# Down by seven block products for eight, with a contraction that rolls over slots

## The chip, the cores and the metric

The kernel runs on one core of a Trainium2 chip. The metric is the device time of one execution in microseconds (us), as the median of several. PE is TensorE (matmuls), DVE is VectorE, ACT is ScalarE, and SyncE's queue (SP) issues the DMAs between the chip's DRAM and its on-chip memory. PE's results land in PSUM, which has eight banks of 512 fp32 columns.

## The reference, cut to what matters

One layer of a streaming encoder, in fp32, for 1024 positions of width 1024. What the change touches is its end, the MLP:

```python
h2 = rms_norm(x, norm2_g)                                        # (1024, 1024)
u = jnp.square(jax.nn.relu(jnp.einsum('bsd,df->bsf', h2, w_up)))  # (1024, 4096)
x = x + jnp.einsum('bsf,fd->bsd', u, w_down)                      # (1024, 1024)
```

I call the product with w_up *up* and the product with w_down *down*.

## The kernel before, in words

Everything lies transposed: channels on the 128 partitions, positions along a row. The stages follow each other on PE: attention with the first gates, the conv branch with the other gates, its projection (cp), the attention's projection (ap), out, up, down. An fp32 product is made from three matmuls: each operand is *cut* into a high part (an ACT cast, `split`, L81) and the rest (a DVE subtraction, L82), and high x high, low x high and high x low add up in one PSUM bank. A matmul has 128 x 128 weights and 512 columns.

The gates, the conv branch and up use *seven block products for eight*. The operand on the right is held in four *slots*; slot j is two tiles of 128 channels by 1024 positions, thus four blocks of 128 x 512, and `slot` makes seven operands of them: blocks 1 to 4 as they are or differences of them. `weights` fetches four weight blocks (a11, a12, a21, a22, 256 KB each), makes sums of them with four DVE operations and cuts seven operands. A product, numbered 1 to 7 and taken in the order 1, 2, 6, 7, 5, 4, 3 (`ORDER`), sums over the four slots: 4 x 3 = 12 matmuls. One job of 84 matmuls yields 256 output channels by 1024 positions. In `product` the first and the last job of a phase are "wide": slot by slot, all seven products side by side in seven banks. The others go product by product in three banks, and ACT or DVE read the banks in between.

Up is 16 jobs (`up_job`). Its results are squared relus, written by DVE and sent to DRAM as 32 tiles uD. Down is plain (`plain`): four quarters of the contraction, each with eight tiles uk loaded from uD (512 KB, through three staging buffers, `bw.stg`) and cut, and eight output tiles, 48 matmuls for each output tile and half-row pair. The quarters are summed in acc by DVE (L1091 to L1107). The last quarter also applies the norm's factor ms and adds to the residual.

The order of the work on each engine is fixed when the program is built: a scheduler lays out each engine's instructions in one queue, and an instruction waits at the head of its queue until its inputs are there and its buffer is free. Buffers come from pools with a fixed count per tag (bufs). SyncE's DMAs stand in one such queue.

Of the kernel before, what the change touches and what calls it, by code (L numbers as in the profile page):

```python
# [8 lines left out]
F32 = mybir.dt.float32  # L9
# [31 lines left out]
def block_kernel(ctx, tc, x, xt, wqkv, wcnv, wgate, wcp, wap, wout, wup, wdown,  # L41
# [135 lines left out]
    h2D = [dram.tile([P, S], F32, name=f"h2D{t}") for t in range(ND)]  # L177
    uD = [dram.tile([P, S], F32, name=f"uD{t}") for t in range(FF // P)]

# [439 lines left out]
    class Work:  # L619


        def __init__(self, name, e, stg, tt, side="right"):
            self.n = (e, stg, tt)
            self.pool = ctx.enter_context(tc.tile_pool(name=name, bufs=1, side=side))

# [3 lines left out]
        def stg(self, name):  # L629
            return self.pool.tile([P, S], F32, name=name, tag="stg", bufs=self.n[1])  # L630
# [44 lines left out]
    def from_dram(tiles, first=0):  # L675
        return lambda dst, kt: nc.sync.dma_start(dst, tiles[first + kt][:])
# [20 lines left out]
    def mms(ps, w, o, i, j, start, stop, chain):  # L697
        x = o[j]
        for n, (u, v) in enumerate(((0, 0), (1, 0), (0, 1))):
            matmul(ps[:], w[i][:, u, j, :], x[:, PROD[i][1], v, :], start and n == 0,  # L700
                   stop and n == 2, chain)
# [5 lines left out]

    def product(src, o, name, ev, wide=None, w=None):


        w = w or weights(src, name)
        if not wide:
            a = bank(f"pa_{name}")

            def whole(ps, i, start, stop):
                for j in range(4):
                    mms(ps, w, o, i, j, start and j == 0, stop and j == 3, True)
            whole(a, 1, True, True)
            if ev.sums:
# [202 lines left out]
    def plain(src, o, name, ev, lead=3, then=None, final=False):  # L922
# [90 lines left out]
    kbs.close()  # L1013
    jls = ExitStack()

    jul = [jls.enter_context(tc.tile_pool(name=f"jul{j}", bufs=1)) for j in range(2)]
    xos = ExitStack()
# [4 lines left out]
    def ev_out(t, c, ps):  # L1022
# [14 lines left out]
        if c == 1 and t in (1, 3):  # L1037
            h2o[t // 2] = slot((jul[t // 2], "js"), t // 2, "n", from_dram(h2D))
    plain(wout, mk, "o", ev_out)
    first = weights(wup[0], "u0")  # L1040
    xos.close()
    kas.close()
    jrs = ExitStack()
    for j in range(2, 4):
        jur = jrs.enter_context(tc.tile_pool(name=f"jur{j}", bufs=1, side="right"))
        h2o[j] = slot((jur, "js"), j, "n", from_dram(h2D))


# [22 lines left out]

    phase([up_job(i) for i in range(16)], h2o, (1, 2, 3, 0), first, 7, mean_square)
    jls.close()
    jrs.close()

    ktd = ctx.enter_context(tc.tile_pool(name="ktd", bufs=1, side="right"))
    acc = [[None] * 2 for _ in range(ND)]

    def ktile(pool, name):
        return pool.tile([P, 2, S], F32R, name=name, tag="kt", bufs=NKD)  # L1080
    NKD = 12
    accp = ctx.enter_context(tc.tile_pool(name="accp", bufs=1))
    acc = [accp.tile([P, S], F32, name=f"acc{t}") for t in range(ND)]
    for k in range(4):
        def uk(k=k):
            return ktiles(ktd, f"uk{k}_", uD, 8 * k)

        def ev_d(t, c, ps):
            a = acc[t][:, cols(c)]
            if k == 0:  # L1090
                nc.scalar.copy(a, ps[:])  # L1091
            elif k < 3:
                nc.vector.tensor_tensor(a, ps[:], a, op=ALU.add)
            if k == 2:

                x2 = bw.e(f"xr{t}_{c}")
                nc.sync.dma_start(x2[:], x2D[t][:, cols(c)])
                nc.vector.tensor_tensor(a, a, ms[:, cols(c)], op=ALU.mult)
                nc.vector.tensor_tensor(a, a, x2[:], op=ALU.add)
            if k == 3:  # L1100
                e = bw.e(f"xl{t}_{c}")
                n = 2 if t == ND - 1 and c else 1
                for q in range(n):
                    f = slice(q * HC // n, (q + 1) * HC // n)
                    g = slice(c * HC + f.start, c * HC + f.stop)
                    nc.vector.tensor_tensor(e[:, f], ps[:, f], ms[:, g], op=ALU.mult)
                    nc.vector.tensor_tensor(e[:, f], e[:, f], acc[t][:, g], op=ALU.add)  # L1107
                    nc.sync.dma_start(out[t * P:(t + 1) * P, g], e[:, f])
        plain(wdown[k], uk if k == 0 else uk(), f"d{k}_", ev_d, 3 if k else 1,
              None, k == 3)  # L1110


def _layout(inputs):
# [53 lines left out]
```

## Time and profile before

| | |
|---|---|
| median of 3 runs | 1810.55 us (1809.3 to 1812.17) |
| the profiled execution | 1811.89 us, span 1810.1 us |
| PE busy | 1785.5 us, 99% of the span |
| DVE busy | 1130.4 us, 62% |
| ACT busy | 695.6 us, 38% |
| up, from the span's start | about 1142 to 1450 us |
| down | about 1450 us to the end |

The span runs from the first to the last instruction on the core; the device time lies some 2 us above it. A row's busy time says what an engine did; an idle time beside it says what it waited for. Where PE is busy throughout, only PE's own rows and PE's waits say what the end depends on.

### The profile page before, as it was taken

To read this page: it belongs to the slowest core of one execution; us is meant where nothing else is said; L and a number is where in the kernel's file an instruction comes from. 1 tells how busy PE (TensorE), PEld (TensorE's weight loads), DVE (VectorE), ACT (ScalarE), POOL (GpSimd) and SP (SyncE) were. 2 spreads that over 40 slices of the span, in tenths; PEclk is the share of its full clock that TensorE was granted. 3 is DMA by queue.
4 is the path that set the end of the run, shared out by engine and by line. 5 is a ranking of instruction groups with operands and counts; after the bars stand their busy time and mean duration, and the time that the engine had idled before them with its cause. 6 is when DMAs were issued, how large, how long until landed. Compare 5 with 4: busy or idle time off the path is not lost.

```text
span 1810.1 us, 24728 instructions
## 1 busy us (share of the span) xinstructions
PE 1785.5 (99%) x8884; PEld 1543.2 (85%) x8884; DVE 1130.4 (62%) x2106; ACT 695.6 (38%) x1337; POOL 151.1 (8%) x419
## 2 busy tenths in 40 slices
PE   7999999999999999999999999999999989999999
PEld 7899999999888888888888888788888878888887
DVE  6777877787759766765543629975765452325532
ACT  6555555565534333333432414433333233212200
POOL 5232223222100000000000000000000000000000
PEclk9999999999999999999999999999999999999999
DMA  7443444433335332213673628543333262424311
GB/s 278 104 114 92 101 109 106 104 102 95 107 108 154 94 99 88 79 57 117 211 235 116 199 75 282 186 150 110 94 127 111 88 223 87 138 68 135 111 64 53
DMA packets 123692, 225.02 MB, mean 124 GB/s; under 512 B 13745, under 2 KB 30385, under 8 KB 123569
## 3 DMA queue, kind: packets, MB, share of 16 engines
q1 hardware_dynamic: 123424, 223.40, 40.2%
q8 instruction: 70, 1.15, 0.3%
q14 instruction: 54, 0.43, 0.1%
q10 hardware_dynamic: 144, 0.03, 0.0%
HBM read 147.88 MB, written 50.33 MB: 110 GB/s over the span
## 4 chain that ended last, share of the span: by engine, by line
PE 90%; DVE 3%; DMA 2%; issue 1%; ACT 0%; SPq 0%; DVEq 0%; ACTq 0%
PE ps_d L74 19%; PE psq L74 13%; PE pa_u L74 8%; PE ps_ap L74 5%; PE ps_cp L74 5%; PE ps_g L74 5%; PE pb_u L74 4%; PE av L74 4%; PE s L74 3%; PE tp L77 3%; PE pa_b L74 2%; PE pa_x L74 2%; PE pa_c L74 2%; PE p_g L74 2%; PE pc_u L74 2%; PE ps_o L74 2%
## 5 line engine op out<-in xcount | busy, mean ns | idle before, releaser
L74 PE MATMUL psq<-w_q,hT 128*128 128x384 f32 x1536 | 347.5, 351 | 9.3 <-ACT w_q L81 6.6
L74 PE MATMUL ps_d<-uk,w_d 128*128 128x512 f32 x1536 | 350.8, 391 | 4.9 <-DVE uk L82 3.9
L74 PEld LDWEIGHTS ps_d<-uk,w_d 128*128 128x128 f32 x1536 | 289.2, 188 | 66.4 <-DVE uk L82 4.7
L74 PEld LDWEIGHTS psq<-w_q,hT 128*128 128x128 f32 x1536 | 261.2, 192 | 12.9 <-ACT w_q L81 6.6
L74 PE MATMUL pa_u<-on,w_u 128*128 128x512 f32 x672 | 160.0, 390 | 0.1
L74 PEld LDWEIGHTS pa_u<-on,w_u 128*128 128x128 f32 x672 | 126.0, 188 | 27.1 <-ACT s_u L705 0.5
L82 DVE TENSOR_TENSOR w_d<-r_d,w_d 128x512 fp32r<-128x512 f32 x64 | 42.7, 687 | 143.4 <-ACT w_d L81 143.3
L400 ACT ACTIVATE p<-p,sm 128x640 f32<-128x640 f32 (+4 forms) x128 | 89.5, 699 | 74.3 <-DVE sm L398 70.5
L81 ACT CAST w_d<-r_d 128x512 fp32r<-128x512 f32 x64 | 38.8, 622 | 168.4 <-PE ps_d L74 160.7
L74 PE MATMUL ps_g<-hT,w_g 128*128 128x512 f32 x384 | 99.6, 398 | 0.7 <-DVE ao L454 0.7
L398 DVE CUSTOM_DVE_ANT_0 p<-s,b 128x640 f32<-128x640 f32 (+4 forms) x128 | 83.3, 651 | 13.0 <-PE s L74 12.6
L82 DVE TENSOR_TENSOR pt<-tp,pt 128x512 fp32r<-128x512 f32 (+1 forms) x144 | 84.2, 596 | 10.4 <-ACT pt L81 9.7
L74 PEld LDWEIGHTS av<-pt,vt 128*128 128x128 f32 x576 | 86.1, 188 | 2.4 <-DVE pt L82 0.6
L74 PE MATMUL av<-pt,vt 128*128 128x256 f32 (+1 forms) x576 | 87.8, 274 | 0.1
L74 PE MATMUL ps_cp<-yk,w_cp 128*128 128x512 f32 x384 | 87.2, 389 | 0.0
L74 PE MATMUL ps_ap<-ak,w_ap 128*128 128x512 f32 x384 | 87.2, 389 | 0.0
L74 PE MATMUL ps_o<-mk,w_o 128*128 128x512 f32 x384 | 87.2, 389 | 0.0
L74 PE MATMUL s<-k,q 128*128 128x384 f32 (+3 forms) x384 | 81.8, 322 | 4.7 <-DMA k<-kh 3.7
L81 ACT CAST pt<-tp 128x512 fp32r<-128x512 f32 (+1 forms) x144 | 71.8, 515 | 37.6 <-PE tp L77 37.3
L74 PEld LDWEIGHTS ps_cp<-yk,w_cp 128*128 128x128 f32 x384 | 72.1, 188 | 15.0
L74 PEld LDWEIGHTS ps_ap<-ak,w_ap 128*128 128x128 f32 x384 | 72.1, 188 | 15.0
L74 PEld LDWEIGHTS ps_o<-mk,w_o 128*128 128x128 f32 x384 | 72.1, 188 | 15.0
(251 smaller groups left out, 2890.4 us busy)
## 6 DMA issues: line engine op xcount, KB each, us to landing
q<-qh SPq DMA_DIRECT2D x128, 128.0 KB, 2.3
r_u_a<-in_wup_dram SPq DMA_DIRECT2D x64, 256.0 KB, 2.8
buk<-uD SPq DMA_DIRECT2D x32, 512.0 KB, 4.7
r_d<-in_wdown_dram SPq DMA_DIRECT2D x64, 256.0 KB, 2.8
r_q<-in_wqkv_dram SPq DMA_DIRECT2D x32, 384.0 KB, 3.5
k<-kh SPq DMA_DIRECT2D x64, 128.0 KB, 2.3
gl<-gD SPq DMA_DIRECT2D x32, 256.0 KB, 3.6
uD<-s_u SPq DMA_DIRECT2D x30, 256.0 KB, 2.9
```

What stands on the lines that cost most here:

```text
L74: pin(nc.tensor.matmul(ps, lhsT, rhs, start=start, stop=stop, skip_group_check=chain))
L77: pin(nc.tensor.transpose(o, i, ident[:]))
L81: return (nc.scalar.copy(hi, src), nc.vector.tensor_tensor(lo, src, hi.bitcast(F32), op=ALU.subtract))
L82: nc.vector.tensor_tensor(lo, src, hi.bitcast(F32), op=ALU.subtract))
L398: nc.vector.tensor_tensor_reduce(pw, sc[:, k0:k1], biast[p, h][:, 5 * P - w:], -1.0, 3e38, ALU.add, ALU.min, sm[:, 0:1])
L400: nc.scalar.activation(pw, pw, AF.Exp, bias=sm[:, 0:1], scale=-1.0, accum_out=sm[:, 1:2])
```

## The change

Down becomes 16 steps of seven block products. The 4096 channels of u are 16 *slots* of 256 channels. Step n works on one of the four pairs of output tiles (pair n % 4) and on the four slots n to n + 3 (counted around after 16), so each pair meets every slot once in four visits. From step to step one slot of operands is replaced: slot n + 4 takes the room of slot n. A slot's seven operands lie in four groups (blocks 0 and 1; 4 and 5; 3 and 6; 2), and a group is replaced as soon as the products that read it are over: group 0 after product 2, group 1 after product 7, group 2 after product 4, group 3 after product 3.

The differences for a slot are now made in up, where its four blocks come out, and written to DRAM with the blocks (uD holds seven blocks per slot). ACT does relu and square there; before, DVE did both in one operation. From slot 4 on, group 0 is also cut in up and written ready-cut (uP, 1 MB), so that down loads it straight into place; its other groups, and all groups of slots 0 to 3, are loaded into staging buffers and cut in down. The last job of up is no longer wide, so that the rooms of the second norm's slots come free group by group, and the first four slots of down are loaded and cut from there on.

The room is found elsewhere: weight operands have 7 buffers for 9; staging has 2 buffers and a third in a pool that lives until the end of out, so that up has 2; down has 4.

The core of the diff:

```diff
-    bw = Work("bw", 4, 3, 3)
+    bw = Work("bw", 4, 2, 3)
...
-    wp = (wk, 9, 5)
+    wp = (wk, 7, 5)
...
+    bw.more = (None, 0)
+    wxs.close()
+    rooms.append(ctx.enter_context(tc.tile_pool(name="jur", bufs=1, side="right")))
...
     def up_job(i):
+        st = {}
         def put(r, c, ps, e):
...
-            nc.vector.scalar_tensor_tensor(e[:], e[:], 0.0, e[:], op0=ALU.max, op1=ALU.mult)
-            nc.sync.dma_start(uD[t][:, cols(c)], e[:])
+            x = st[r, c]
+            nc.scalar.activation(x, total(ps, e)[:], AF.Relu)
+            nc.scalar.square(x, x)
...
+                if parted(i):
+                    hl = ux.tile([P, 2, 2, HC], F32R, name=f"uh{i}", tag="hl")
+                    split(hl[:, :, 0], hl[:, :, 1], st["g"][:])
+                    nc.sync.dma_start(uP[i][:], hl[:].bitcast(F32))
...
+                for o, y, z in ((d2[:, 0], st[0, 1], st[0, 0]), (d1[:, 0], st[1, 1], d2[:, 0]),
+                                (d1[:, 1], st[1, 1], st[0, 1]), (d2[:, 1], st[1, 0], d1[:, 0])):
+                    nc.vector.tensor_tensor(o, y, z, op=ALU.subtract)
+                nc.sync.dma_start(uD[i][:, 2:4], d1[:])
+                nc.sync.dma_start(uD[i][:, 4:6], d2[:])
...
+    def load_group(n, g):
+        i = n % NS
+        if g == 0 and parted(i):
+            return None
+        x = bw.stg(f"bu{n}_{g}").rearrange("p (a q) -> p a q", a=2)[:, :GROUPS[g]]
+        nc.sync.dma_start(x, uD[i][:, 2 * g:2 * g + GROUPS[g]])
+        return x
+
+    def make_group(n, g, x):
+        o = so.setdefault(n, [None] * 4)
+        o[g] = group_room(n, g, f"ou{n}_{g}")
+        if x is None:
+            gate(nc.sync.dma_start(o[g][:].bitcast(F32), uP[n % NS][:]))
+        else:
+            for ins in split(o[g][:, :, 0], o[g][:, :, 1], x):
+                gate(ins)
+
+    LEFT = {2: 0, 7: 1, 4: 2, 3: 3}
+
+    def first_slots(i):
+        if i in LEFT:
+            for n in range(4):
+                make_group(n, LEFT[i], load_group(n, LEFT[i]))
-    phase([up_job(i) for i in range(16)], h2o, (1, 2, 3, 0), first, 7, mean_square)
+    phase([up_job(i) for i in range(NS)], h2o, None, first, 7, mean_square, first_slots)
...
+    bw.more = (accp, 2)
...
+    def down_step(n):
+        p, v = n % 4, n // 4
+        w = weights(wdown[n], f"d{n}")
+        o = [so[n + d] for d in range(4)]
+        new = {}
+        if n + 4 < NS + 3:
+            for g in range(4):
+                new[g] = load_group(n + 4, g)
+
+        def whole(ps, i, start, stop):
+            for j in range(4):
+                mms(ps, w, o, i, j, start and j == 0, stop and j == 3, True)
+            if new and i in LEFT:
+                make_group(n + 4, LEFT[i], new[LEFT[i]])
...
+        a = bank(f"pa_d{n}")
+        whole(a, 1, True, True)
+        s1 = snap(a, f"s1_d{n}")
+        c = bank(f"pc_d{n}")
+        whole(c, 2, True, True)
+        sums(0, 0, c[:], s1)
+        whole(a, 6, False, True)
...
+    for n in range(NS):
+        down_step(n)
```

`snap` copies a bank on ACT, `sums` adds a visit's results into acc on DVE (three operations in a pair's first visit, seven in the second, nine in the third, thirteen in the last; the factor ms and the residual come in with the last two). The weight array wdown is laid out anew to fit the steps.

How the instructions stand, at three places. Names: ps_d, pa_d and pc_d are PSUM banks of down, pa_u and p1 to p7 of up, w_ are cut weights, r_ raw ones, on cut operands of the second norm, uk (before) and ou (now) cut operands of down, buk and bu their staging buffers, with slot and group as in bu3_1; x2 and x3 are repeats.

PE where up ends and down begins, before: the last job's products side by side, then down's first output tile, both halves of a row for each tile uk.

```order
L74 MATMUL p4_u15_13790<-on0_11077,w_u15_4_13764 128x512 x3
L74 MATMUL p3_u15_13794<-on0_11077,w_u15_3_13767 128x512 x3
L74 MATMUL ps_d0_0_0_13953<-uk0_0_13911,w_d0_0_0_13903 128x512 x3
L74 MATMUL ps_d0_0_1_13957<-uk0_0_13911,w_d0_0_0_13903 128x512 x3
L74 MATMUL ps_d0_0_0_13953<-uk0_1_13916,w_d0_0_1_13906 128x512 x3
L74 MATMUL ps_d0_0_1_13957<-uk0_1_13916,w_d0_0_1_13906 128x512 x3
```

The same place now: product 3 of the last job, then product 1 of down's step 0.

```order
L75 MATMUL pa_u15_13983<-on2_3_11598,w_u15_3_13980 128x512 x3
L75 MATMUL pa_u15_13983<-on3_3_11628,w_u15_3_13980 128x512 x3
L75 MATMUL pa_d0_14236<-ou0_0_14013,w_d0_1_14203 128x512 x3
L75 MATMUL pa_d0_14236<-ou1_0_14018,w_d0_1_14203 128x512 x3
L75 MATMUL pa_d0_14236<-ou2_0_14023,w_d0_1_14203 128x512 x3
L75 MATMUL pa_d0_14236<-ou3_0_14028,w_d0_1_14203 128x512 x3
```

Before, PE begins down with one operand tile and takes the next only after six matmuls; now its first twelve matmuls want the first group of all four slots.

SyncE's queue at the same place, before: loads of uk tiles, up's last results and a residual (xr).

```order
L916 DMA buk0_3_13924<-uD3_166 128x1024
L916 DMA buk0_4_13929<-uD4_167 128x1024
L1056 DMA uD30_193<-s1_u15_13861 128x512
L1097 DMA xr0_0_15177<-x2D0_147 128x512
L1056 DMA uD31_194<-u2_u15_13863 128x512
L1056 DMA uD30_193<-u4_u15_13864 128x512
L1056 DMA uD31_194<-u5_u15_13871 128x512
L916 DMA buk0_5_13934<-uD5_168 128x1024
```

The same place now, first where group 0 and 1 of the four slots are loaded:

```order
L1145 DMA bu2_0_14021<-uD2_165 128x1024
L1145 DMA bu3_0_14026<-uD3_166 128x1024
L94 DMA r_d1_a11_14346<-in_wdown_dram 128x512
L94 DMA r_d1_a12_14348<-in_wdown_dram 128x512
L1145 DMA bu0_1_14064<-uD0_163 128x1024
L94 DMA r_d1_a21_14350<-in_wdown_dram 128x512
L1145 DMA bu1_1_14069<-uD1_164 128x1024
L94 DMA r_d1_a22_14352<-in_wdown_dram 128x512
L1103 DMA uD15_178<-ud15_14032 128x512
L1145 DMA bu2_1_14074<-uD2_165 128x1024
L1145 DMA bu3_1_14079<-uD3_166 128x1024
```

and some rows later, where the last group of slots 0 to 3 and the groups of slots 4 and 5 are loaded:

```order
L1145 DMA bu1_3_14158<-uD1_164 128x512
L1145 DMA bu2_3_14163<-uD2_165 128x512
L94 DMA r_d2_a12_14499<-in_wdown_dram 128x512
L1145 DMA bu5_2_14383<-uD5_168 128x1024
L94 DMA r_d2_a21_14501<-in_wdown_dram 128x512
L1145 DMA bu5_3_14385<-uD5_168 128x512
L1145 DMA bu3_3_14168<-uD3_166 128x512
L1145 DMA bu4_3_14234<-uD4_167 128x512
```

Fourteen such loads of slots 0 to 3 stand in the queue from up's last job on, in the order of the groups (bu0_0 and bu1_0 stand far ahead, among up's first jobs), each behind the one that had its buffer; bu3_3, the last, stands behind two loads of slot 5. The buffer of bu5_3 is that of bu4_2.

SyncE's queue where out ends and up begins, before:

```order
L676 DMA bn3_0_11611<-h2D6_161 128x1024
L93 DMA r_u2_a11_11890<-in_wup_dram 128x512
L93 DMA r_u2_a12_11892<-in_wup_dram 128x512
L1027 DMA x2D7_154<-x7_0_11520 128x512
L1027 DMA x2D7_154<-x7_1_11532 128x512
L1031 DMA h2D7_162<-h7_0_11524 128x512
L1031 DMA h2D7_162<-h7_1_11536 128x512
L676 DMA bn3_1_11613<-h2D7_162 128x1024
```

The same place now; h2D are the second norm's tiles, bn2 and bn3 the staging buffers for slots 2 and 3.

```order
L94 DMA r_u2_a11_11927<-in_wup_dram 128x512
L1060 DMA x2D7_154<-x7_0_11526 128x512
L1060 DMA x2D7_154<-x7_1_11538 128x512
L1064 DMA h2D7_162<-h7_0_11530 128x512
L1064 DMA h2D7_162<-h7_1_11542 128x512
L707 DMA bn3_0_11621<-h2D6_161 128x1024
L707 DMA bn3_1_11623<-h2D7_162 128x1024
```

bn3_0 has moved behind the last tile's results, and with two staging buffers bn3_0 and bn3_1 take those of bn2_0 and bn2_1.

## Rows read from the trace of the kernel before

**Rows 1.** The page, part 1: busy us (share of the span) and instructions
```profile
PE 1785.5 (99%) x8884; PEld 1543.2 (85%) x8884; DVE 1130.4 (62%) x2106; ACT 695.6 (38%) x1337; POOL 151.1 (8%) x419
```

**Rows 2.** Windows: us, busy us of PE, PEld, DVE, ACT, POOL, PEclk, DMA share, GB/s
```profile
1142.40:1447.00 304.60, 304.22 (x1336) 250.22 (x1335) 203.30 (x310) 103.53 (x182) 0.00 (x0) 1.00 0.36 118
1447.00:1464.00 17.00, 12.48 (x46) 9.20 (x44) 13.83 (x19) 6.58 (x8) 0.00 (x0) 0.90 0.74 239
1464.00:1806.00 342.00, 341.21 (x1504) 282.21 (x1504) 129.78 (x183) 70.73 (x102) 0.00 (x0) 1.00 0.32 104
```

**Rows 3.** Chain of waits: start us, length us, what; up's end, down's start
```profile
1403.80 2.72 PE pa_u L74 x12
...
1449.39 4.63 DMA buk<-uD
1456.60 5.43 DMA buk<-uD
```

**Rows 4.** Timeline of PE at down's start: start us, length, what [idle before]
```profile
1449.87 3.33 PE L74 MATMUL ps_d<-uk,w_d 128*128 128x512 f32 x14
1456.54 5.53 PE L74 MATMUL ps_d<-uk,w_d 128*128 128x512 f32 x16 [3.34 <-DVE uk L82]
1463.15 0.74 PE L74 MATMUL ps_d<-uk,w_d 128*128 128x512 f32 x2 [1.07 <-ACT uk L81]
1464.41 5.97 PE L74 MATMUL ps_d<-uk,w_d 128*128 128x512 f32 x25 [0.52 <-DVE uk L82]
```

**Rows 5.** Groups by form, PE, down: count | busy us, mean ns | idle before
```profile
L74 PE MATMUL ps_d<-uk,w_d 128*128 128x512 f32 x1536 | 350.8, 391 | 4.9 <-DVE uk L82 3.9 <-ACT uk L81 1.1
```

**Rows 6.** Windows behind the wait of 3.34 us
```profile
1456.50:1458.00 1.50, 1.46 (x4) 1.15 (x5) 1.50 (x2) 0.00 (x0) 0.00 (x0) 0.69 1.00 365
1458.00:1459.50 1.50, 1.50 (x5) 1.22 (x4) 1.50 (x3) 0.00 (x0) 0.00 (x0) 0.50 1.08 266
...
1461.00:1462.50 1.50, 1.08 (x5) 0.55 (x3) 0.00 (x0) 0.45 (x1) 0.00 (x0) 1.00 1.00 360
```

**Rows 7.** Staging tile buk (512 KB): durations ns min/median/max, landings us
```profile
L81 ACT CAST uk<-buk x32: 1044/1052/1057, 1445.3 to 1714.8; 128x1024 fp32r<-128x1024 f32 x32
L82 DVE TENSOR_TENSOR uk<-buk,uk x32: 1216/1224/1227, 1446.4 to 1715.9; 128x1024 fp32r<-128x1024 f32 x32
...
DMA to landing us min/median/max: 3.2/4.7/6.1
```

**Rows 8.** The same view of r_d, raw weights of down (256 KB)
```profile
L81 ACT CAST w_d<-r_d x64: 611/622/633, 1428.4 to 1761.5; 128x512 fp32r<-128x512 f32 x64
L82 DVE TENSOR_TENSOR w_d<-r_d,w_d x64: 677/685/694, 1429.0 to 1762.1; 128x512 fp32r<-128x512 f32 x64
...
DMA to landing us min/median/max: 2.4/2.8/6.0
```

**Rows 9.** Timeline of SyncE's queue where up begins
```profile
1140.11 0.33 SPq L676 DMA_DIRECT2D bn<-h2D  x1
...
1150.56 0.32 SPq L676 DMA_DIRECT2D bn<-h2D  x1
```

**Rows 10.** Timeline of DVE there
```profile
1151.73 0.68 DVE L82 TENSOR_TENSOR on<-tn,on 128x512 fp32r<-128x512 f32 x1
1152.33 0.68 DVE L663 TENSOR_TENSOR tn<-bn,tn 128x512 f32<-128x512 f32 x1
```

**Rows 11.** Timeline of PE there
```profile
1159.69 2.56 PE L74 MATMUL p_u<-on,w_u 128*128 128x512 f32 x10 [0.24 <-DVE on L82]
```

**Rows 12.** Groups by form in up: a bank's copy, an activation, a reciprocal
```profile
L705 ACT COPY s_u<-pa_u 128x512 f32<-128x512 f32 x14 | 8.2, 587 | 26.1 <-PE pa_u L74 22.8 <-DMA uD<-s_u 3.3
...
L1070 DVE RECIPROCAL rb<-rb 128x512 f32<-128x512 f32 x2 | 6.6, 3322 | 0.0
...
L1035 ACT ACTIVATE x<-x 128x512 f32<-128x512 f32 x2 | 1.3, 632 | 2.5 <-DMA x2D<-x 2.2 <-DVE on L82 0.3
```

**Rows 13.** Timeline of DVE at down's start: three cuts back to back
```profile
1455.27 3.49 DVE L82 TENSOR_TENSOR uk<-buk,uk 128x1024 fp32r<-128x1024 f32 x3
```

More of the change, by code (lines that the diff above doesn't have):

```diff
@@ L177, in block_kernel @@
     h2D = [dram.tile([P, S], F32, name=f"h2D{t}") for t in range(ND)]
-    uD = [dram.tile([P, S], F32, name=f"uD{t}") for t in range(FF // P)]
+    uD = [dram.tile([P, 7, HC], F32, name=f"uD{i}") for i in range(NS)]
+    uP = [dram.tile([P, 2, 2, HC], F32, name=f"uP{i}") for i in range(NS)]
     def row_load(pool, st, parts=1, then=None):
@@ L629, in stg @@
         def stg(self, name):
-            return self.pool.tile([P, S], F32, name=name, tag="stg", bufs=self.n[1])
+            own = self.n[1]
+            self.turn = (self.turn + 1) % (own + self.more[1])
+            pool, n = (self.pool, own) if self.turn < own else self.more
+            return pool.tile([P, S], F32, name=name, tag="stg", bufs=n)
         def tt(self, name):
             return self.pool.tile([P, HC], F32, name=name, tag="tt", bufs=self.n[2])
-    bw = Work("bw", 4, 3, 3)
+    bw = Work("bw", 4, 2, 3)
     wk = ctx.enter_context(tc.tile_pool(name="wk", bufs=1, side="right"))
+    wxs = ExitStack()
+    wx = wxs.enter_context(tc.tile_pool(name="wx", bufs=1, side="right"))
+    bw.more = (wx, 1)
     jss = ExitStack()
@@ L647, in etile, with group_room, operand @@
         return bw.e(name)
+    POS = {0: (0, 0), 1: (0, 1), 4: (1, 0), 5: (1, 1), 3: (2, 0), 6: (2, 1), 2: (3, 0)}
+    GROUPS = (2, 2, 2, 1)
+    def group_room(j, g, name):
+        return rooms[j % 4 // 2].tile([P, GROUPS[g], 2, HC], F32R, name=name,
+                                      tag=f"o{j % 4}_{g}")
+    def operand(o, k, v):
+        if isinstance(o, list):
+            g, n = POS[k]
+            return o[g][:, n, v, :]
+        return o[:, k, v, :]
     def slot(pool, j, name, fetch):
@@ L699, in mms @@
         for n, (u, v) in enumerate(((0, 0), (1, 0), (0, 1))):
-            matmul(ps[:], w[i][:, u, j, :], x[:, PROD[i][1], v, :], start and n == 0,
+            matmul(ps[:], w[i][:, u, j, :], operand(x, PROD[i][1], v), start and n == 0,
                    stop and n == 2, chain)
@@ L1013, in block_kernel @@
     kbs.close()
-    jls = ExitStack()
-    jul = [jls.enter_context(tc.tile_pool(name=f"jul{j}", bufs=1)) for j in range(2)]
+    rooms = [ctx.enter_context(tc.tile_pool(name="jul", bufs=1))]
     xos = ExitStack()
@@ L1042, in block_kernel, with parted @@
     kas.close()
-    jrs = ExitStack()
+    bw.more = (None, 0)
+    wxs.close()
+    rooms.append(ctx.enter_context(tc.tile_pool(name="jur", bufs=1, side="right")))
+    uxs = ExitStack()
+    ux = uxs.enter_context(tc.tile_pool(name="ux", bufs=1))
     for j in range(2, 4):
-        jur = jrs.enter_context(tc.tile_pool(name=f"jur{j}", bufs=1, side="right"))
-        h2o[j] = slot((jur, "js"), j, "n", from_dram(h2D))
+        h2o[j] = slot(None, j, "n", from_dram(h2D))
+    def parted(i):
+        return i >= 4
@@ L1084, in block_kernel @@
[L1084 to L1088, printed above, removed]
-            a = acc[t][:, cols(c)]
[L1090 to L1104, printed above, removed]
+    so = {}
@@ new lines, in block_kernel, with plus, scaled, residual @@
+    bw.more = (accp, 2)
+    def plus(o, x, y):
+        nc.vector.tensor_tensor(o, x, y, op=ALU.add)
+    def scaled(o, x, f):
+        nc.vector.tensor_tensor(o, x, ms[:, f], op=ALU.mult)
+    def down_step(n):
[11 more added lines that the diff above has]
+                make_group(n + 4, LEFT[i], new[LEFT[i]])
+        xr = {}
+        def residual(r):
+            t = 2 * p + r
+            xr[r] = bw.stg(f"x2_{t}")
+            nc.sync.dma_start(xr[r][:], x2D[t][:])
+        def sums(r, c, x, y):
+            t = 2 * p + r
+            a = acc[t][:, cols(c)]
+            if v == 3 and r == 0:
+                e = y or etile(f"l{t}_{c}")
+                if y:
+                    plus(e[:], x, e[:])
+                q = 2 if n == NS - 1 and c else 1
+                for k in range(q):
+                    f = slice(k * HC // q, (k + 1) * HC // q)
@@ new lines, in sums @@
+            if v == 0:
+                if y:
+                    plus(a, x, y[:])
+                else:
+                    nc.scalar.copy(a, x)
+            else:
+                if y:
+                    plus(a, a, y[:])
+                plus(a, x, a)
+            if v == 3:
+                scaled(a, a, cols(c))
+                plus(a, a, xr[r][:, cols(c)])
+                nc.sync.dma_start(out[t * P:(t + 1) * P, cols(c)], a)
+        if v == 3:
+            residual(1)
+        a = bank(f"pa_d{n}")
@@ new lines, in down_step @@
+        whole(a, 1, True, True)
[4 more added lines that the diff above has]
+        whole(a, 6, False, True)
+        u2 = snap(a, f"u2_d{n}")
+        b = bank(f"pb_d{n}")
+        whole(b, 7, True, True)
+        s7 = snap(b, f"s7_d{n}")
+        whole(a, 5, False, True)
+        u4 = bw.tt(f"u4_d{n}")
+        nc.scalar.copy(u4[:], a[:])
+        sums(1, 1, u4[:], s7)
+        whole(b, 4, False, True)
+        sums(1, 0, b[:], u2)
@@ L1113, in _layout @@
+        if v == 2:
+            residual(0)
+        whole(a, 3, False, True)
+        sums(0, 1, a[:], None)
+        if v == 2:
+            t = 2 * p
+            scaled(acc[t][:], acc[t][:], slice(0, S))
+            plus(acc[t][:], acc[t][:], xr[0][:])
+    for n in range(NS):
+        down_step(n)
 def _layout(inputs):
```

74 lines of the change are left out of this document (46 added, 28 removed).

## The prediction

> **What bounds the kernel now.** I read four views in this order. First the page's busy times: TensorE (PE) is busy for 1785.5 of 1810.1 us, and no other engine passes 62% [rows 1]. Then the stretches by stage: up and down, the two stages that change, are nearly all PE work, while VectorE (DVE) and ScalarE (ACT) are busy for two thirds of the time or less. The exception is the first 17 us of down, where PE works only 12.48 us [rows 2]. Then the chain of waits: it runs from matmul block to matmul block, twelve matmuls in 2.72 us, and leaves PE only at down's start, for two loads of buk [rows 3]. So a matmul less is 2.72 / 12 = 0.2267 us less, and a wait counts only where PE stands still. Last, PE's own rows at down's start: waits of 3.34, 1.07 and 0.52 us, 4.9 together [rows 4].
>
> **The change part by part.** A block product is 12 matmuls, so a step of seven is 84 matmuls or 19.04 us.
>
> *Removed.* Down has 1536 matmuls [rows 5]. Sixteen steps of 84 are 1344, so 192 go: 192 x 0.2267 = **43.5 us less**. Up keeps its count; its last job only takes the other order. The 4.9 us of waits at down's start go with the loads that caused them. [...] Together **6.8 us less**.
>
> *Added: the first four slots.* Down's step 0 needs all four slots, 16 groups, and every group is loaded from DRAM into a staging buffer and cut in two (an ACT cast and a DVE subtraction) before PE reads it. In up's last job only two staging buffers are left. The first two groups lie in them long before; the other 14 go through in rounds: landing, cast, subtraction, then the next load. For 512 KB the rows give a landing of 4.7 us (3.2 to 6.1), a cast of 1.05 and a subtraction of 1.22 [rows 7]: 7.0 us a round (5.5 to 8.4). I count from the start of up's last job. Product 2 ends at 5.44 and frees the first rooms. The first buffer's group is cut by 5.44 + 1.05 + 1.22 = 7.7, and the second's, whose subtraction follows, by 8.9. The second buffer then carries the groups 3_0, 1_1, 3_1, 1_2 and 3_2 (slot_group), five rounds: 3_2 is ready at 8.9 + 5 x 7.0 = 43.9. PE wants it for the last quarter of product 5, with no wait at 19.04 + 4 x 2.72 + 2.04 = 31.96. That is a **wait of 11.9 us** (4.4 at the fast round, 18.9 at the slow one). It swallows the waits for group 1 before it.
>
> Product 4 ends 0.68 + 2.72 us after that, and product 3 wants the last group, 3_3. On the SyncE queue its load stands behind bu5_3, whose buffer is free only after slot 4's group 2 is cut, and that cut needs product 4 to be over. So from the end of product 4: 1.05 + 1.22 for that cut, 0.65 for two issues, 2.8 for a load of 256 KB (2.4 to 6.0), and 0.62 + 0.69 for the cut [rows 8] = 7.0. PE is there after 2.04: a **wait of 5.0 us** (4.6 to 7.7, the last with the 5.5 us of a busy stretch).
>
> *Clock.* Both waits are longer than the 3.34 us after which the trace shows slow matmuls. I take 1.9 us for each, **3.8 us** (nothing to 5.7, three falls). [...]
>
> *Out to up.* Slots 2 and 3 of the second norm now share two staging buffers instead of three. The last load (bn3_1) went out at 1150.56 [rows 9]; now it must wait until bn2_1 was last read, by the subtraction at 1152.33 to 1153.0 [rows 10]: 2.4 us later. That chain was the one PE waited for, 0.24 us at 1159.69 [rows 11]. VectorE fills part of the delay with slot 2's cuts, so I take **1.0 us** (0 to 2.4).
>
> *Taken at nothing.* Up's epilogue: ACT has 7 casts, 3 copies, 8 activations and one cast of 1024 a step, 4.35 + 1.76 + 5.0 + 1.05 = 12.2 us of 19.04 at the durations of [rows 7, 8, 12]. DVE starts an operation every 0.60 us, one of 1024 every 1.14 [rows 10, 13]: 18 x 0.60 + 1.14 = 11.9. In the step after the mean square two reciprocals of 3.3 us [rows 12] and six more make 22.1, so DVE falls back 3 us; the weights, cut up to 16 us ahead, hide it, and without that cover it is 3 us. Fewer weight buffers (7 for 9): a product's buffer is free one step before it is wanted, 16.3 us for a cut of 1.3; without that cover 1.3 us a product. Slot replacement in steady state: a group's room is free 5.75 products, 15.6 us, before PE wants it again, and the loads lie ahead in four staging buffers; the 1 MB that comes ready cut costs 9.4 us (two 512 KB landings). DMA: 3.3 MB a step against 2.1 in up, where the engines are 36% busy [rows 2]. Down's DVE: 11 operations for weights, 3 x 1.14 + 0.60 for groups and 13 for sums in the heaviest steps (12 to 14) are 18.4 us of 19.04: full, but not over.
>
> The sum: -43.5 - 6.8 + 11.9 + 5.0 + 3.8 + 1.0 = -28.6 us. It is made against the profiled execution, 1811.89 us with a span of 1810.1; that gives 1783.3. The median of the runs shown, 1810.55, lies 1.3 lower, so I predict **1782 us**.
>
> **The rivals.**
>
> *The first loads are well hidden* (14%). At the smallest landing, 3.2, the first wait is 4.4 and the second 4.6, the clock stays up, and up's start costs nothing: -50.3 + 9.0 = -41.3, **1769 us**. For it: two transfers at a time, where the waits of rows 4 had more in flight. Against it: the same stretch also carries weights, up's last blocks and slots 4 and 5.
>
> *The DMA engines are saturated there* (10%). At down's start the trace has a DMA share of 1.00 at 365 GB/s [rows 6]. In about 45 us the change moves some 15 MB there (7.3 for the sixteen groups, 3 of weights, 2.4 of up's last blocks, 2.6 for slots 4 and 5), 330 GB/s. If every 512 KB takes 6.1, the terms are 18.9 + 7.7 + 5.7 + 2.4 - 50.3 = -15.6: **1795 us**.
>
> *VectorE bounds down's last steps* (9%). If it were occupied by an operation for its whole duration, 0.69 (1.22), steps 12 to 14 would need 25 x 0.69 + 3 x 1.22 = 20.9 us of DVE against 19.04 of PE: three times 1.9, so **1788 us**. [...] The trace bears it out little: three operations of 1024 end 3.49 us after the first began, not 3.67 [rows 13].
>
> *The slot replacement is late in every step* (4%, the slower side). The ready-cut megabyte is issued only when product 2 has freed its room, and the weights of two steps on stand behind it in SyncE's queue. If what stands before it takes a 512 KB landing as well, and each takes the longest seen, it arrives after 18.3 us where 15.6 are covered. That is 2.7 us in each of the twelve steps that load one, 32 us: **1814 us**. It decides from about 2.7 us a step on. For it: the saturated stretch. Against it: steady down would move 3.3 MB in 19 us, about half of what the engines have shown.
>
> **How the numbers follow.** My forecast has 60%, by itself 1776 to 1790. The rivals have 14, 10, 9 and 4%, and 3% stay for about no change. A measurement here can tell 0.2%, 3.6 us. Faster by more holds the forecast and the first three rivals, 93%; within it 3%; slower 4%. The range 1771 to 1795 takes in the forecast, the saturated and the VectorE case and most of the hidden one.
>
> **What would show it.** In the profile after: down's groups hold 1344 matmuls of 512 columns, still 2.72 us a dozen. PE's waits stand almost all in step 0, some 12 us in product 5 for slots 2 and 3 and 5 us in product 3 for the fourth slot, each released by the cut of a staged group (ou), with a granted clock below 1 right behind. Steps 1 to 15 show no wait above 1 us, DVE is about 18 of 19 us busy near the end, and the tail after the last matmul stays. Waits of PE in every step, or for weights, would prove me wrong; so would a step 0 without a wait above 3 us.

## The result, and the profile after

The kernel after takes **1783.97 us** (median of four runs, 1782.1 to 1785.6) against 1811.19 before in the same comparison: a ratio of **0.985** with the interval [0.9835, 0.986]. Predicted were 1782 us and a range of 1771 to 1795. Its profiled execution took 1783.33 us with a span of 1781.5, which is 28.6 us less than that of before; the sum in the prediction was also 28.6. The sum came out, but some of its terms are off in both directions, and one had the wrong reason.

The page, part 1: busy us, share of the span, instructions (compare [rows 1]).

```profile
PE 1747.8 (98%) x8692; PEld 1506.2 (85%) x8692; DVE 1262.7 (71%) x2290; ACT 855.1 (48%) x1597; POOL 152.8 (9%) x419
```

PE has 192 instructions fewer. DVE has 132 us more work and ACT 160. In down PE waits for them at its start alone: the idle time of the next groups is all in step 0. PE's groups of down: count | busy us, mean ns | idle before, and what ended it (compare [rows 5]).

```profile
L75 PE MATMUL pa_d<-ou,w_d 128*128 128x512 f32 x768 | 188.6, 396 | 12.8 <-ACT ou L82 8.6 <-DVE ou L83 3.0 <-ACT s_d L736 1.2
L75 PE MATMUL pb_d<-ou,w_d 128*128 128x512 f32 x384 | 94.0, 394 | 0.0
L75 PE MATMUL pc_d<-ou,w_d 128*128 128x512 f32 x192 | 46.1, 389 | 0.0
```

768 + 384 + 192 = 1344. Idle time rose from 4.9 to 12.8 us, and nearly all of it waits for ou, the cut groups. PE's timeline over step 0: start us, length, what, idle before (compare [rows 4]).

```profile
1433.43 2.88 PE L75 MATMUL pc_u<-on,w_u 128*128 128x512 f32 x12
...
1448.14 3.02 PE L75 MATMUL pa_u<-on,w_u 128*128 128x512 f32 x12 [0.94 <-DVE s_u L836]
1450.99 2.88 PE L75 MATMUL pa_d<-ou,w_d 128*128 128x512 f32 x12
...
1457.81 2.90 PE L75 MATMUL pa_d<-ou,w_d 128*128 128x512 f32 x11 [1.22 <-ACT s_d L736]
...
1472.92 2.05 PE L75 MATMUL pa_d<-ou,w_d 128*128 128x512 f32 x3 [3.08 <-ACT ou L82]
1476.68 2.05 PE L75 MATMUL pa_d<-ou,w_d 128*128 128x512 f32 x3 [1.70 <-ACT ou L82]
1478.53 4.61 PE L75 MATMUL pb_d<-ou,w_d 128*128 128x512 f32 x12
1482.98 1.30 PE L75 MATMUL pa_d<-ou,w_d 128*128 128x512 f32 x5
1485.66 1.20 PE L75 MATMUL pa_d<-ou,w_d 128*128 128x512 f32 x4 [1.38 <-DVE ou L83]
1489.12 5.23 PE L75 MATMUL pa_d<-ou,w_d 128*128 128x512 f32 x15 [2.26 <-ACT ou L82]
1494.19 1.08 PE L75 MATMUL pc_d<-ou,w_d 128*128 128x512 f32 x4
```

The threes at 1472.92 and 1476.68 are product 5 for slots 2 and 3, the row at 1478.53 is product 4, the fifteen at 1489.12 begin with product 3 for group 3_3. The row of pc_u is product 2 of up's last job, which thus began 2.72 us earlier, at 1430.71. I use one yardstick for all kernels below: the time from there to step 1's product 2 (here 1494.19). It is 63.48 us; without a stall it is 15 products, 40.80. **Step 0's loss is 22.7 us.** Windows of the same stretch (us, busy us of PE, PEld, DVE, ACT, POOL, PEclk, DMA share, GB/s; compare [rows 2, 6]):

```profile
1451.00:1466.00 15.00, 12.48 (x52) 8.88 (x50) 13.11 (x18) 10.50 (x16) 0.00 (x0) 1.00 0.87 263
1466.00:1480.00 14.00, 7.33 (x14) 3.73 (x15) 6.29 (x8) 5.61 (x7) 0.00 (x0) 0.59 0.86 318
1480.00:1494.00 14.00, 10.36 (x34) 7.56 (x33) 9.59 (x14) 5.80 (x10) 0.00 (x0) 0.80 0.77 234
```

From 1466 to 1480 PE, DVE and ACT all stand idle for about half of the time, while the DMA engines are 86% busy. Are they the limit, or the buffers that they fill? The experiments turn on that. The staged loads of this stretch (landings in us; compare [rows 7]):

```profile
L83 DVE TENSOR_TENSOR ou<-bu,ou x19: 684/1224/1226, 1437.3 to 1491.5; 128x1024 fp32r<-128x1024 f32 x14, 128x512 fp32r<-128x512 f32 x5
L82 ACT CAST ou<-bu x18: 617/1044/1060, 1435.6 to 1490.2; 128x1024 fp32r<-128x1024 f32 x13, 128x512 fp32r<-128x512 f32 x5
...
DMA to landing us min/median/max: 2.7/4.6/6.5
```

This view mixes loads of 512 and 256 KB. The ten 512 KB loads that go out for slots 0 to 3 from 1438 us on took 3.5 to 6.5 us, 4.8 in the mean.

Behind step 0 the trace shows no wait of PE at all. Two windows of down, a step in the first visit and one in the last (same columns):

```profile
1507.96:1527.00 19.04, 19.04 (x85) 15.77 (x85) 12.30 (x17) 9.30 (x15) 0.00 (x0) 1.00 0.56 179
1736.44:1755.48 19.04, 19.04 (x85) 15.77 (x85) 18.95 (x30) 9.88 (x15) 0.00 (x0) 1.00 0.65 212
```

A step takes 19.04 us, as worked out; DVE is 18.95 us busy in the last and still holds nothing up.

### The profile page after: what moved, and what is told of

It is laid out like the page before. It is cut to its first block, busy times and chain, and to the rows that moved or that the text cites. A ratio compares the mean times of both kernels' runs of the same rounds, so it can differ in the third digit from the quotient of the medians.

```text
span 1781.5 us, 24912 instructions
## 1 busy us (share of the span) xinstructions
PE 1747.8 (98%) x8692; PEld 1506.2 (85%) x8692; DVE 1262.7 (71%) x2290; ACT 855.1 (48%) x1597; POOL 152.8 (9%) x419
## 4 chain that ended last, share of the span: by engine, by line
PE 87%; DVE 4%; DMA 4%; ACT 1%; issue 1%; SPq 0%; DVEq 0%; ACTq 0%
PE psq L75 12%; PE pa_d L75 9%; PE pa_u L75 9%; PE ps_ap L75 5%; PE ps_cp L75 5%; PE ps_g L75 5%; PE pb_d L75 5%; PE pb_u L75 4%; PE av L75 3%; PE s L75 3%; PE tp L78 3%; PE pa_b L75 2%; PE pa_x L75 2%; PE pa_c L75 2%; PE pc_d L75 2%; PE pc_u L75 2%
## 5 line engine op out<-in xcount | busy, mean ns | idle before, releaser
L75 PE MATMUL pa_d<-ou,w_d 128*128 128x512 f32 x768 | 188.6, 396 | 12.8 <-ACT ou L82 8.6
L75 PEld LDWEIGHTS pa_d<-ou,w_d 128*128 128x128 f32 x768 | 145.3, 190 | 48.6 <-ACT ou L82 11.0
L75 PE MATMUL pa_u<-on,w_u 128*128 128x512 f32 x720 | 171.5, 390 | 0.9 <-DVE s_u L836 0.9
L75 PEld LDWEIGHTS pa_u<-on,w_u 128*128 128x128 f32 x720 | 135.0, 188 | 30.0 <-DVE s_u L836 1.4
L75 PE MATMUL pb_d<-ou,w_d 128*128 128x512 f32 x384 | 94.0, 394 | 0.0
L75 PEld LDWEIGHTS pb_d<-ou,w_d 128*128 128x128 f32 x384 | 73.5, 191 | 15.5
L75 PE MATMUL pb_u<-on,w_u 128*128 128x512 f32 x360 | 86.5, 389 | 0.0
```

Of the source, the lines that this page charges most:

```text
L75: pin(nc.tensor.matmul(ps, lhsT, rhs, start=start, stop=stop, skip_group_check=chain))
```

## The experiments

All are edits of the kernel after, and its 1784.0 us is what they are read against; the yardstick is from each one's own trace.

**1. Fewer staged groups.** `parted(i)` is true for every slot, so group 0 of slots 0 to 3 too comes ready-cut.

```diff
-        return i >= 4
+        return True
```

> Group 0 of slots 0 to 3 is cut inside up as well and comes as one ready-cut 1 MB load, so that 12 instead of 16 groups go through the two staging buffers behind up. In the changed kernel the wait for the third cut group of product 5 of step 0 and the one for product 3 cost 14.0 + 4.1 us and the slow clock around them 4.6 us. Staging theory (two buffers, a group in and out of each in 7 us): three rounds instead of four and more stand before that group, it is ready about 7 to 8 us earlier, the waits of product 5 fall to 6 us or less, and the time is 1775 to 1778 us (6 to 9 us less than 1784). Rival, the DMA engines are full there (busy share 0.87 from 1451 to 1480 us): the ready-cut loads bring twice the bytes of the staged ones (1 MB for 512 KB), nothing is ready earlier, and the time is 1782 to 1786 us with the same waits. Rival, the cuts on ScalarE and VectorE: four cuts fewer, each group about 2 us earlier, 1780 to 1782 us.

Measured: **1778.2 us**, ratio to before 0.9816 [0.9801, 0.9831], 0.2 us above the range expected. Step 0's loss is 16.8 us, 5.9 less. The waits of product 5 are 5.1 us together, the longest 2.05, and its third group came 4.6 us earlier, not 7 to 8:

```profile
1465.14 0.73 PE L75 MATMUL pa_d<-ou,w_d 128*128 128x512 f32 x2 [2.05 <-ACT ou L82]
...
1468.89 4.15 PE L75 MATMUL pa_d<-ou,w_d 128*128 128x512 f32 x6 [1.99 <-ACT ou L82]
```

The bytes of group 0 doubled and a megabyte took 8.2 us (median). Beside more transfers a landing did take longer: the two staged loads issued beside the four megabytes took 10.7 and 10.8 us, at a DMA share of 0.89 from 1431 to 1451, where the ten of the kernel after took 3.5 to 6.5. Yet with more bytes the groups came earlier, which is not what a stretch bound by the DMA engines would show.

**2. Three staging buffers.**

```diff
+    bw.more = (ux, 1)
...
-                st[1, 1] = ux.tile([P, HC], F32, name=f"ud{i}", tag="b22", bufs=2)[:]
+                st[1, 1] = ux.tile([P, HC], F32, name=f"ud{i}", tag="b22", bufs=1)[:]
```

(and the same for b12)

> Three instead of two buffers for the groups that are cut behind up; up's own buffers for one sum and one difference go from two to one to make the room. Staging theory: three groups in 7 us instead of two, the third cut group of product 5 is ready by 31 us after the start of up's last job, when it is due at 32, the loads of slot 3 stand ahead of those of slot 5 in SyncE's queue, and of the 22.7 us lost in step 0 some 15 to 20 go: 1764 to 1769 us, unless up pays for its single buffers (each wait there would show on the matmuls of up). Rival, DMA full: a landing takes half as long again, 10 us a round, the waits stay within 3 us of where they are, and the time is 1780 to 1786 us. Rival, the wait moves: the weights of up or of step 1 are late instead because their loads stand behind the new ones in SyncE's queue, 1773 to 1780 us.

Measured: **1776.9 us**, 0.9807 [0.9792, 0.9821]. Both theories hold a part. Step 0's loss fell from 22.7 to 5.2 us (1435.28 to 1481.25 is 45.97), within the 15 to 20 expected. But up's last job began 4.6 us later (its first had taken 3.9 longer), and step 1's product 6 waited for weights: with the slow matmuls behind it 5.8 us. -17.5 + 4.6 + 5.8 = -7.1, as measured. PE's rows of step 0 and 1 there:

```profile
1471.14 0.50 PE L75 MATMUL pa_d<-ou,w_d 128*128 128x512 f32 x1 [0.72 <-DVE ou L83]
1471.47 2.90 PE L75 MATMUL pb_d<-ou,w_d 128*128 128x512 f32 x12
1474.21 4.92 PE L75 MATMUL pa_d<-ou,w_d 128*128 128x512 f32 x21
1480.45 0.97 PE L75 MATMUL pa_d<-ou,w_d 128*128 128x512 f32 x3 [1.31 <-DMA ou<-uP]
1481.25 2.91 PE L75 MATMUL pc_d<-ou,w_d 128*128 128x512 f32 x12
1487.35 0.49 PE L75 MATMUL pa_d<-ou,w_d 128*128 128x512 f32 x1 [3.19 <-ACT w_d L82]
```

Products 5, 4 and 3 run through, with the same bytes loaded. With three loads under way the 512 KB loads of slots 0 to 3 took 3.6 to 6.4 us, hardly longer than with two (3.5 to 6.5). The number of buffers, not the DMA engines, had set the rounds.

**3. No landings.** One staged group, loaded once, is cut into all 16 places of slots 0 to 3; 15 loads are left out.

```diff
...
-                make_group(n, LEFT[i], load_group(n, LEFT[i]))
+                make_group(n, g, one["x"][:, :GROUPS[g]])
```

> One staged group is loaded once and all 16 groups of slots 0 to 3 are cut from it: the other 15 loads of 512 KB are left out, so step 0 and those that use these slots compute with the wrong columns; every cut and every matmul stays. Staging theory (what is late are the landings, each of which needs a buffer back first): the waits for cut groups in products 5 and 3 go but for the ready-cut loads of slot 4 and the chain of cuts, 10 to 20 us less than 1784: 1764 to 1774 us. Rival, the cuts on ScalarE and VectorE set the rounds: the cuts come no faster than now, the third group of product 5 stays within 3 us of its 46 us from the start of up's last job, 1780 to 1784 us.

Measured: **1769.3 us**, 0.9764 [0.9749, 0.9778]. No wait for a cut group is left; all cuts are still made, so ScalarE and VectorE did not set the rounds. The loss of 8.1 us is mostly another wait, for a bank's copy (s_d) that stands on ACT behind cuts of groups and of weights, and the slow matmuls after it:

```profile
1458.57 5.25 PE L75 MATMUL pa_d<-ou,w_d 128*128 128x512 f32 x12 [4.11 <-ACT s_d L736]
```

**4. PE kept busy in the waits.**

```diff
+    BUSY = {(0, 5, 2): 12, (0, 5, 3): 10, (0, 3, 3): 8}
...
+                for _ in range(BUSY.get((n, i, j), 0)):
+                    matmul(dm[:], w[5][:, 0, 0, :], w[5][:, 0].rearrange("p a q -> p (a q)"),
+                           True, True, True)
```

> Thirty matmuls whose results nobody reads are added in step 0: 12 ahead of the third and 10 ahead of the fourth group of product 5, 8 ahead of the fourth group of product 3, where TensorE now waits 3 and 2 us at a time. Clock theory (the matmuls behind the waits ran at the low granted clock because TensorE had been idle, 4.6 us lost): the granted clock stays at 1.00 through product 5 and the time falls by 2 to 4.6 us, to 1779 to 1782 us. Rival, these matmuls are slow for another reason than the idle time before them: the clock falls all the same, and the added matmuls cost what doesn't fit into the waits, 1784 to 1788 us.

Measured: **1783.6 us**, 0.984 [0.9823, 0.9858]: no change. The clock did rise, in the midst of the added matmuls (dm); from 1466 to 1480 us it was 0.88 where it had been 0.59:

```profile
1470.76 4.14 PE L75 MATMUL dm<-w_d 128*128 128x512 f32 x12
1474.74 0.84 PE L75 MATMUL pa_d<-ou,w_d 128*128 128x512 f32 x3
1475.42 2.43 PE L75 MATMUL dm<-w_d 128*128 128x512 f32 x10
1477.68 0.86 PE L75 MATMUL pa_d<-ou,w_d 128*128 128x512 f32 x3
1478.38 2.92 PE L75 MATMUL pb_d<-ou,w_d 128*128 128x512 f32 x12
...
1489.59 5.57 PE L75 MATMUL pa_d<-ou,w_d 128*128 128x512 f32 x15 [2.07 <-ACT ou L82]
```

Product 4 took 2.92 us instead of 4.61 and was over 1.3 us earlier, counted from the start of up's last job. But 3_3 came 59.4 us after that start (58.4 in the kernel after), so the wait for it took the gain back. Its load went out 0.7 us earlier and then took 4.46 us to land instead of 2.79. Whether the added matmuls had a part in that is not shown. In this trace PE also entered down 2.5 us later, behind a longer wait at up's end (1.88 us for s_u), which the waits of step 0 swallowed. So this run shows that the clock can be held up, but not what a fast clock is worth.

**5. The third buffer only from up on.** As experiment 2, with `bw.more = (ux, 1)` set behind the loads of the second norm.

> Three staging buffers as in the run before, but the third is handed out only after the loads of the second norm, so that these have the two buffers of the changed kernel. With the third buffer from the start, step 0's loss fell from 22.7 to 5.2 us, but up's first job took 4.2 us longer and step 1 waited 5.8 us for weights: 1776.9 us. Theory: the 4.2 us at up's start came from that buffer alone and go, the gain in step 0 and the loss in step 1 stay: 1772 to 1773.5 us. Rival, the loss at up's start has another cause (up's single buffers): 1776 to 1778 us. Rival, the gain in step 0 hung on the other order of the buffers: 1778 to 1782 us.

Measured: **1772.3 us**, 0.9788 [0.9774, 0.9803]. Up's first job is no longer than in the kernel after (20.3 us, from 1142.17 to 1162.44, for 21.0), step 0's loss is 5.0, and step 1 waits as in experiment 2. The theory holds.

**6. The same, with step 1's weights ahead.**

```diff
...
+        if n == 0:
+            early[n + 1] = raws(wdown[n + 1], f"d{n + 1}")
```

(`raws` issues the four loads, ahead of `load_group` for slot 4)

> As the other kernel of this call with three staging buffers, and the loads of step 1's weights are written ahead of slot 4's and 5's, so that the fourth of them (a22) is issued right behind the last group of slot 3, 5 us or more earlier. Queue theory (that load stood behind loads that wait for rooms): step 1's wait of 5.8 us falls to 2 or less and the time is 1767 to 1769.5 us. Rival, VectorE's order: the sums of the weights stand behind subtractions that wait for landings of slot 4, so an earlier load changes little: 1771.5 to 1773 us.

Measured: **1770.8 us**, 0.9778 [0.9764, 0.9793]: between the two, and the interval overlaps that of experiment 5. The wait for weights is gone, as queue theory says, but PE now waits longer for the ready-cut megabyte of slot 4, which stands behind staged loads (1.96 us in experiment 5):

```profile
1479.48 1.65 PE L75 MATMUL pa_d<-ou,w_d 128*128 128x512 f32 x3 [5.03 <-DMA ou<-uP]
1480.92 4.21 PE L75 MATMUL pc_d<-ou,w_d 128*128 128x512 f32 x12
```

**7. 3_3's load ahead of slot 5's.** Two buffers again, one edge more in SyncE's queue.

```diff
...
+        if n == 5:
+            tc.add_manual_dep(d.ins, so["d"].ins.name, ...)
```

(`so["d"]` is the load of 3_3)

> The changed kernel with one edge in SyncE's queue: the loads of slot 5 go behind the load of slot 3's last group (3_3); buffers, bytes and work are the same. Queue theory (3_3 is late because it stands behind a load that waits for slot 4's group 2, cut after product 4): 3_3 is loaded 4 us or more earlier, the wait for it (4.1 us) and the slow clock behind it (1.7 us) go, and the time is 1778 to 1780 us. Rival, the rounds of landings set it: the wait falls by less than 1.5 us, 1782.5 to 1785 us. The waits of product 5 stay as they are by both.

Measured: **1783.7 us**, 0.9851 [0.9835, 0.9868]. The time is in the rival's range. The queue theory, a step of my prediction, falls: 3_3 comes 58.7 us after the start of up's last job. DVE's rows, then SyncE's:

```profile
1483.37 0.69 DVE L1176 TENSOR_TENSOR acc<-pb_d,u_d 128x512 f32<-128x512 f32 x1 [1.67 <-PE pb_d L75]
1483.98 2.42 DVE L83 TENSOR_TENSOR ou<-bu,ou 128x1024 fp32r<-128x1024 f32 x3
```

```profile
1478.67 0.90 SPq L94 DMA_DIRECT2D r_d_a<-in_wdown_dram  x2
1485.83 4.49 SPq L1145 DMA_DIRECT2D bu<-uD  x5
```

3_3's buffer is that of 1_3. The cut of 1_3 is one of the three subtractions at 1483.98, and on DVE they stand behind a sum that reads product 4's bank. The load of 3_3, the first of the five at 1485.83, goes out as the cut of 1_3 ends. So it does in the kernel after (1485.63), with a load of slot 5 ahead of it on SyncE.

**8. The same with 14 matmuls in the waits** of product 5 (8 and 6, as in experiment 4).

> As the run with the edge in SyncE's queue, and 14 matmuls whose results nobody reads: 8 ahead of the third group of product 5 of step 0 and 6 ahead of the fourth, in the waits there. With the same idea alone the clock rose and the time stayed, since the wait for 3_3 took back what product 5 gained. Theory: with that wait gone the slow clock of product 5 is on the path, and the added matmuls give 1.5 to 3 us against the run with the edge alone (1775.5 to 1778 if that is 1779). Rival, the added matmuls cost as much at the low clock as they give: within 1 us of it.

Measured: **1782.1 us**, 0.9841 [0.9826, 0.9855]. 1.6 us less than experiment 7, inside the theory's 1.5 to 3, but the intervals overlap. The traces say the same: a loss of 21.8 us against 23.1. Its premise (the wait for 3_3 gone) did not hold.

**9. 3_3 freed from product 4.** Besides the edge of experiment 7, the cuts of 1_3, 2_3 and 3_3 go ahead of that sum or of the cut of slot 4's group 2, and the loads of step 2's weights go behind 3_3's load.

```diff
+                    if n == 0 and (r, c) == (1, 0):
+                        behind(d, so["cut", 1][1])
...
```

> In the run with the edge in SyncE's queue the wait for slot 3's last group stayed, and its trace shows why the edge was not enough: its buffer is that of group 1_3, whose cut stands on ScalarE behind the cut of slot 4's group 2 and on VectorE behind that and a sum of product 4, which all wait for product 4. Here the cuts of 1_3, 2_3 and 3_3 go ahead of these, and the loads of slot 5 and of step 2's weights behind 3_3's load. Theory: product 4 no longer matters; 3_3 then is ready two rounds of a 256 KB group (issue 0.3, landing 3.0, cut 0.62 + 0.69) behind 3_2's cut, 2 us before the 58.4 us after the start of up's last job at which it was, and the time is 1781 to 1782.5 us. Rival, the landings alone set it: no change, 1783 to 1785 us.

Measured: **1780.6 us**, 0.983 [0.9816, 0.9843], a little under the expected 1781 to 1782.5. The interval overlaps that of the kernel after; the trace is clearer: step 0's loss is 20.7 us for 22.7. 3_3 comes 56.4 us after the start of up's last job, 2.0 earlier than in the kernel after, and DVE's rows show the cut of 1_3 first, the sum behind it:

```profile
1482.19 0.69 DVE L83 TENSOR_TENSOR ou<-bu,ou 128x512 fp32r<-128x512 f32 x1
1482.80 0.68 DVE L1185 TENSOR_TENSOR acc<-pb_d,u_d 128x512 f32<-128x512 f32 x1
```

PE's row of 3_3:

```profile
1486.39 5.25 PE L75 MATMUL pa_d<-ou,w_d 128*128 128x512 f32 x15 [1.75 <-ACT ou L82]
```

**10. The best: experiment 6 with the ready-cut megabyte ahead of slot 4's staged loads.**

```diff
+            for b in late if n == 4 else ():
+                tc.add_manual_dep(b.ins, d.ins.name, ...)
```

> The kernel with three staging buffers and early weights of step 1, and one edge more in SyncE's queue: the ready-cut megabyte of slot 4 goes ahead of slot 4's staged loads. There PE waited 5.03 us for that megabyte in step 1's product 1, with 1.9 us of slow clock behind it. Queue theory (it stood behind staged loads that wait for buffers): the wait falls to 0 to 2.5 us and the time to 1765 to 1768.5 us. Rival, the transfer itself is late (DMA share 0.89 there, 6 to 8 us a megabyte): the wait stays above 4 us, or moves to the staged groups of slot 4, 1769.5 to 1771.5 us.

Measured: **1764.8 us** (1762.7 to 1768.6), 0.9739 [0.9725, 0.9753]: 19 us below the kernel after and 47 below the one before. What is left of PE's waits in down, in the trace of its slowest execution (1768.6):

```profile
L75 PE MATMUL pa_d<-ou,w_d 128*128 128x512 f32 x768 | 184.3, 392 | 3.3 <-ACT s_d L738 1.9 <-DMA ou<-uP 0.9 <-DVE ou L83 0.4
```

## Why the prediction was right, and where its steps were not

*The matmuls, -43.5: right.* 1344 are left, a step takes 19.04 us.

*The old start of down, -6.8: 7.3.* The 33rd matmul began at 1464.41 [rows 4]; from 1449.87 it was due at 1457.12. My 6.8 were 4.9 of waits and 1.9 of slow clock: the 16 matmuls behind the wait of 3.34 us took 5.53 us, where 16 x 0.2267 are 3.63 [rows 4], at a granted clock of 0.50 from 1458.0 to 1459.5 and of 1.00 again from 1461.0 [rows 6].

*The wait for 3_2, +11.9: 14.0.* PE reached 3_2 in product 5 at 1476.68, 45.97 us after the start of up's last job, where 31.96 was due. The mechanism is right and shown by experiments 1 to 3 (losses of 16.8, 5.2 and 8.1 us in step 0 for 22.7): landings in rounds through two buffers. The second buffer's group was cut at 8.9 us, as worked out; DVE's row below begins with 3_2's subtraction, so the fifth round ended 1.22 later, 47.2 after the start. A round took (47.2 - 8.9) / 5 = 7.65 us and not 7.0, in all 3.3 us more. The loads of this buffer took 5.5, 3.5, 4.0, 5.5 and 6.5 us to land, 5.0 in the mean where I had 4.7: that is 1.4 of the 3.3. Another 1.6 are the round of 1_1 alone, whose cast and subtraction stood ready but waited for their turn on ACT and DVE, for which I had set nothing. The rest is the short gaps from one engine to the next. The loads themselves went out as soon as their buffer was free. Of the 3.3 us PE gets 1.2 back by starting on the high part. 3_2's load, cast and subtraction:

```profile
1469.02 6.40 SPq L1145 DMA_DIRECT2D bu<-uD  x4
```

```profile
1475.58 1.04 ACT L82 CAST ou<-bu 128x1024 fp32r<-128x1024 f32 x1 [2.71 <-DMA bu<-uD]
```

```profile
1476.66 1.83 DVE L83 TENSOR_TENSOR ou<-bu,ou 128x1024 fp32r<-128x1024 f32 x2 [2.53 <-ACT ou L82]
```

*The wait for 3_3, +5.0: 4.1, for a partly wrong reason.* From product 4's end it took 6.1 us, not 7.0. I put it on SyncE's queue and on a cut that needs product 4 to be over. That cut (slot 4's group 2) did not need it: its cast began at 1481.58, before product 4's end at 1482.98. Experiment 7 shows that the queue's order alone changed nothing (1783.7 us for 1784.0), and experiment 9 that product 4 came in through the order on VectorE: a sum of its bank stood ahead of the cut that frees 3_3's buffer. Even freed, 3_3 came only 2.0 us earlier, because two rounds stand between it and 3_2 (10.35 us in experiment 9).

*The clock, +3.8: 4.6 long, what it cost stays open.* The rows at 1476.68, 1478.53 and 1489.12 are 1.17, 1.73 and 1.67 us longer to the next start than their matmuls need; the granted clock was 0.59 in the window of 1466 to 1480. That each long wait brings a slow clock with it was my estimate from the one wait of before. The trace agrees for the longer waits: behind that of 3.08 us three matmuls took 2.05 us (0.68 at 0.2267 each), behind that of 2.26 fifteen took 5.23 (3.40). Behind that of 1.22 us it hardly shows: eleven took 2.90 (2.49). Not all of the 4.6 us need be on the path: experiment 4 got nothing back, and experiment 8 1.6 us, which its intervals do not set apart from nothing. In experiment 4 the fifteen behind the last wait stayed slow (5.57 us), so what their 1.67 us are worth is not shown.

*Out to up, +1.0: 1.1, and nothing in the end.* Up's first job took 20.99 us, not 19.89; but it began 0.94 us earlier (1141.26, not 1142.20), which I had not foreseen. The traces of experiments 1 and 3 to 10 have that start anywhere from 1139.3 to 1142.2, so the 0.94 is within their scatter. Their first jobs took 20.3 to 22.9 us, all longer than before. The reason that I gave, two staging buffers for three, is not shown: experiment 2 gave these loads a third buffer again, and its first job took 24.9. Up's last job began 0.12 us earlier than before.

*Not foreseen:* waits of 0.94 and 1.22 us for copies and sums of banks (s_u, s_d) that stand behind cuts on ACT and DVE. Here they are swallowed by the wait for 3_2. Experiment 3 shows 4.1 us for the second, once the landings are gone.

The new sum by the trace is -43.5 - 7.3 + 22.7 - 0.1 = -28.2, and the time from the last matmul to the end is 0.2 us shorter: -28.4 of the measured -28.6. That my own sum met it to the tenth is luck: +2.1 and +0.8 of the stalls stand against -0.9 there, -1.1 at up's start and -0.9 in the rest.

*The rivals.* Well hidden: wrong for this kernel, but experiment 10, at 1764.8, goes below what it would have given (1769), by other buffers and orders. Saturated DMA: the share was 0.86 and a 512 KB load took 4.8 us in the mean, not 6.1; experiment 2 moved the same bytes with 17.5 us less loss, and experiment 1 moved more. VectorE as the bound of steps 12 to 14: the window above has DVE at 18.95 of 19.04 us where this rival asked for 20.9, and no wait of PE. Late replacement in each step: no wait of PE behind step 0.

## What to carry to other kernels

Where a stage needs many operands at once, count the rounds through the staging buffers (landing, cut, and the queues between them) against the time at which each operand is due: here a third buffer took 17.5 of 22.7 us out of step 0. After that the order in each queue decided, one queue at a time (1772.3, 1770.8, 1764.8 us in experiments 5, 6 and 10): each mended wait let the next one show (weights, then the ready-cut megabyte). An edge on one queue did nothing (1783.7 us for 1784.0) as long as the same wait stood on another engine. What the slow clock cost hung on the waits behind it: matmuls added to keep the clock up ended product 4 1.3 us earlier in experiment 4, which the wait for 3_3 took back, and gave 1.6 us in experiment 8, which the noise covers.

## What the runs showed of the hardware that was not expected

DMA engines that were 86% busy in a window were not what held it up: with a third buffer, at 0.88 to 0.90, the same loads came in time (298 to 308 GB/s from 1451 to 1480, against 263 to 318), and a 512 KB load took 5.1 us in the mean with three under way, against 4.8 with two. Beside four loads of a megabyte it took 10.7 and 10.8 (experiment 1). And PE's granted clock came back while it ran matmuls that nobody needed (0.88 from 1466 to 1480, where it had been 0.59), and stayed up for those behind them: 0.84 us for three, where they had taken 2.05 (experiment 4).
